# A fused decoder block in float32 on one core: the second feed-forward's output product by seven block products of 2x2 blocks, and two of the four weight sums of each block made by accumulating transfers

## The chip, the cores and the metric

The kernel runs on one core of one Trainium2 chip. The metric is the device time of one execution in microseconds (us). Three timed executions gave 1016.72, 1017.11 and 1018.24 us; the median, 1017.11 us, is the time before.

## What is computed

One decoder layer on 512 positions of width 1024, in float32. Cut to what matters here:

```python
def swiglu(u, w_in, w_out):
    a, b = jnp.split(u @ w_in, 2, axis=-1)
    return (jax.nn.silu(a) * b) @ w_out
...
u = modulate(rmsnorm(h, g_norm_ffn1[l]), sh1, sc1)
h = h + 0.5 * gt1 * swiglu(u, w_ffn1_in[l], w_ffn1_out[l])
u = modulate(rmsnorm(h, g_norm_mix[l]), sh2, sc2)
h = h + gt2 * token_mixing(u, cos, sin, ...)
u = modulate(rmsnorm(h, g_norm_ffn2[l]), sh3, sc3)
h = h + 0.5 * gt3 * swiglu(u, w_ffn2_in[l], w_ffn2_out[l])
return rmsnorm(h, g_final)
```

The nine shifts, scales and gates come from `silu(c) @ w_ada`, 72 blocks of 128 values; VectorE computes most of them beside the first feed-forward and the mixing layer, from transfers of 512 KB. The feed-forward's inner width is 2816, which is 22 inner tiles of 128.

## The kernel before

Everything is kept transposed, features on the 128 partitions and the 512 positions on the free axis. Every operand of a matrix product is split into a high part (the value rounded to the matmul's fp32r format by ScalarE) and a low part (the rest, by VectorE), and each product of 128x128 weights is three matmuls: high by high, high by low and low by high.

**Weights.** They come from HBM in chunks of 128x1024 float32 (512 KB), in one order for the whole kernel (`plan`: the list `loads` says what is transferred, the list `order` in which order chunks are split and used). `fetch` (L215) issues transfers on SyncE's queue (SP) into raw buffers: three (`raw0` to `raw2`), and two more, `rawx`, which are halves of the tile X that become free in the middle of the first block of each feed-forward. `split_hi` (L271) lets ScalarE write the chunk's high part into a ring `whi` (L294); `split_lo` (L300) lets VectorE write the low part into `wlo` (L306) and gives the raw buffer free. The ring holds about seven chunks. `look(4)` (L315) is called ahead of each product and splits chunks up to the fourth one after the chunk that the product takes, so four splits stand in the queues of ScalarE and VectorE ahead of what follows the product.

**The first products of a feed-forward.** `ffn_pair` computes the two halves (a and b) of one inner tile with 24 matmuls of 512 columns each; the first feed-forward does tiles 4 to 7 so (0 to 3 are done at the start), the second tiles 0 to 3 (`PLAIN`). Further tiles go in twos through `duo` (L723), by seven block products in place of eight: the weights of two tiles are four blocks of 128x1024 (W11, W12, W22, W21; each is two tiles by half of the 1024 rows), the input u is cut into four blocks too (half of the rows by half of the positions), and sums of blocks are multiplied. The sums of u are made once (`u_steps`); the sums of weights are made for every block by VectorE, four subtractions of 128x1024 each (`make`, L240). In the list `order` a block of weights is seven entries, called e0 to e6 below. `product` (L712) does one of the seven: 24 matmuls of 256 columns. The products 0, 2, 4 and 6 accumulate in the same PSUM bank A; after product 0 ScalarE copies A to bank C, after products 2 and 4 to SBUF (L726), and the next product into A has to wait for that copy. `step` runs work that was put off (`later`) by a number of products.

**The output of a feed-forward** (`ffn`). The 22 inner tiles are five parts (`PARTS`): four of four tiles and a last one of six. After a part's tiles (and, in most parts, the first duo of the next part, `pairs_before`) the kernel multiplies them by the output weights: four chunks, two of the eight output tiles each, 96 matmuls of 512 columns, and adds each to H with the gate (L863). In the first feed-forward VectorE works at blocks of `w_ada` beside this (`bg`, L360), and their transfers into the tiles cs and AR stand in SP's queue between those of the weights (L352).

A part of four tiles in the second feed-forward is so two duos of seven products and an output of four chunks. `H`, `HI`/`HK` (high and low part of the inner tiles) and the input's `UH`/`UL` lie in SBUF.

Of the kernel before, what the change touches and what calls it, by code (L numbers as in the profile page):

```python
# [55 lines left out]
def lay_ffn(w_in, w_out, first, plain):  # L56

    ins, outs = [], []  # L60
    if first:
        cols = np.concatenate([c for j in range(first) for c in _tiles(j * P, DFF + j * P)])
        for k in range(KT):
            ins.append(w_in[k * P:(k + 1) * P][:, cols])
    for j in range(first, plain):
        for c in _tiles(j * P, DFF + j * P):
            ins.append(_fmajor(w_in, c))
    for j in range(plain, FT, 2):
        for i, c in ((0, 0), (0, DFF), (1, DFF), (1, 0)):
            rows = w_in[i * D // 2:(i + 1) * D // 2]  # L70
            ins.append(np.concatenate([_fmajor(rows, x) for x in _tiles(c + j * P, c + j * P + P)], axis=1))
    for k0, k1 in PARTS:
        for m in range(KT):
            outs.append(_fmajor(w_out[k0 * P:k1 * P], np.arange(m * P, (m + 1) * P)))
    n = KT * (len(PARTS) - 1)
    return ins, [np.concatenate(outs[i:i + 2], axis=1) for i in range(0, n, 2)] + outs[n:]
# [60 lines left out]
class Kernel:  # L137
# [6 lines left out]
    def plan(self):  # L144
# [21 lines left out]
        def blocks(recs):  # L166
            n = len(self.loads)
            self.shifted.update(range(len(self.order), len(self.order) + 7))
            self.loads.extend(recs)
            r11, r12, r22, r21 = (("raw", n + i) for i in range(4))  # L170
            x0, x1 = ("x", 0), ("x", 1)
            for need, src, make in ((0, r11, None), (1, x0, (x0, r12, r11)), (2, x1, (x1, r22, x0)), (3, r21, None),
                                    (3, r12, (r12, r22, r12)), (3, r22, None), (3, x0, (x0, r21, x1))):
                for j, x in enumerate((r11, r12, r22, r21)):
# [8 lines left out]
        def ffn(n, ins, outs, first):  # L183
# [4 lines left out]
            for part, (k0, k1) in enumerate(PARTS):  # L188
# [9 lines left out]
                plain(outs[part * KT // 2:(part + 1) * KT // 2] if part + 1 < len(PARTS) else outs[-KT:])  # L198
# [16 lines left out]
    def fetch(self, n=None):  # L215

        n = len(self.order) - 1 if n is None else min(n, len(self.order) - 1)
        while self.fetched <= self.order[n][1] and self.free:
            i = self.fetched
            name, off, w = self.loads[i]  # L220
            src = self.a[name][off:off + P * w].rearrange("(p n) -> p n", p=P)
# [12 lines left out]
    def make(self, i):  # L234

        while self.made <= i:
            m = self.order[self.made][3]
            if m:
                out, x, y = (self.source(z) for z in m)
                self.nc.vector.tensor_tensor(out, x, y, op=OP.subtract)  # L240
# [400 lines left out]
    def ffn_post(self, j, s, pb):  # L641
        nc = self.nc
        h = self.fw.tile([P, T], F32, name=("hf", "u3")[j % 2])
# [5 lines left out]
    def ffn_silu(self, j, pa):  # L649
        s = self.fw.tile([P, T], F32, name=("sl", "u2")[j % 2])  # L650
# [22 lines left out]
    def u_steps(self, n):  # L673
# [18 lines left out]
        def whole(u, k):  # L692
# [5 lines left out]
        return ([whole(a11, 0), whole(a12, 4)] if n else []) + [add(a22, a21, a22, OP.add), split(0, a22), add(a21, a11, a21, OP.subtract), split(2, a21),  # L698
                add(a11, a22, a11, OP.subtract), split(1, a11), add(a12, a12, a11, OP.subtract)], last
# [23 lines left out]
    def duo(self, j, first, last):  # L723
# [13 lines left out]
        c = self.fw.tile([P, 2 * T], F32, name="hf")  # L737
        u2, u3, p5 = (self.fw.tile([P, T], F32, name=x) for x in ("u2", "u3", "p5"))
        q = lambda x: x.rearrange("p (j h t) -> p j h t", j=2, h=2)
        r = lambda x: x.rearrange("p (j t) -> p j t", j=2)  # L740
        silu = lambda h, bank: nc.scalar.activation(q(s)[:, :, h, :], r(bank), AF.Silu)
# [4 lines left out]
        def high():  # L746
            copy(self.HHall[:, j % NH * T:(j % NH + 2) * T], c)

        def low():
            x = slice(j % NH * T, (j % NH + 2) * T)  # L750
            v.tensor_tensor(self.HLall[:, x], c, self.HHall[:, x], op=OP.subtract)


        for i, (bank, u, start) in enumerate(((A, blk(lo4, T1), True), (B, S[0], True), (A, S[1], False),
                                              (C, blk(hi4, T1), False), (A, S[2], False), (B, S[3], False),
                                              (A, blk(hi4, T2), False))):
            if i == 6:
                v.tensor_tensor(q(c)[:, :, 1, :], r(u3), r(p5), op=OP.add)
# [8 lines left out]
            elif i == 1:  # L767
                copy(p5, B)
            elif i == 2:
                copy(u2, A)  # L770
            elif i == 3:
                silu(0, C)
            elif i == 4:
                copy(u3, A)
            elif i == 6:
                silu(1, A)
                v.tensor_tensor(q(c)[:, :, 0, :], r(B), r(u2), op=OP.add)
# [8 lines left out]

    def ffn2(self):
        self.put, self.now = [], 0
        bk = [self.nb() for _ in range(4)]
        self.head(2, bk, AF.Silu)  # L790
        self.todo, last = self.u_steps(2)
# [33 lines left out]
    def ffn(self, n, j, last=None):  # L825
# [10 lines left out]
        for part, (k0, k1) in enumerate(PARTS):  # L836
            tail = part + 1 == len(PARTS)
            while j < pairs_before(n, part):
# [3 lines left out]
                else:  # L842
                    self.duo(j, last, tail and j + 2 == FT)
# [5 lines left out]
            hk = [(self.HH[k % NH], self.HL[k % NH]) for k in range(k0, k1)]  # L849
            if not tail:  # L850
# [494 lines left out]
    def build(self):  # L1345
# [39 lines left out]
        with self.open_ffn():  # L1385
            self.ada_pool = ExitStack()
            self.adaw = self.ada_pool.enter_context(tc.tile_pool(name="f1a", bufs=4))
            self.put, self.now = [], 0
# [135 lines left out]
def lay_inputs(x, c, positions, w_ada, b_ada, g_norm_ffn1, w_ffn1_in, w_ffn1_out, g_norm_mix, w_in, w_pool,  # L1524
# [4 lines left out]
    f1i, f1o = lay_ffn(A(w_ffn1_in)[0], A(w_ffn1_out)[0], FIRST, PLAIN[0])  # L1529
    f2i, f2o = lay_ffn(A(w_ffn2_in)[0], A(w_ffn2_out)[0], 0, PLAIN[2])  # L1530
# [33 lines left out]
```

## Time and profile before

| what | value |
|---|---|
| median of three timed executions | 1017.11 us (1016.72 to 1018.24) |
| span of the profiled execution, first to last instruction | 1018.4 us |
| busy: TensorE (PE), VectorE (DVE), ScalarE (ACT), GpSimd (POOL) | 1007.5, 756.1, 437.2, 26.2 us |
| mean granted TensorE clock | 0.997 |
| the second feed-forward, from its first inner tile of 512 columns to the last part | 691 to 973 us |

The profiled execution's own time is its span, 1018.4 us, 0.13% over the median of the timed ones. PE is the row of matmuls; a matmul's busy time overlaps the next one's, so that the spacing of the starts, not the mean duration, is what one costs. In a row of a group stand the line, the engine, the operation, the tiles out<-in, the shapes and the count; then busy us and mean ns; then the idle time of the engine just before them and what ended it. SPq is the queue of transfers that SyncE issues.

### The profile page before, as it was taken

To read this page: it belongs to the slowest core of one execution; us is meant where nothing else is said; L and a number is where in the kernel's file an instruction comes from. 1 tells how busy PE (TensorE), PEld (TensorE's weight loads), DVE (VectorE), ACT (ScalarE), POOL (GpSimd) and SP (SyncE) were. 2 spreads that over 40 slices of the span, in tenths; PEclk is the share of its full clock that TensorE was granted. 3 is DMA by queue.
4 is the path that set the end of the run, shared out by engine and by line. 5 is a ranking of instruction groups with operands and counts; after the bars stand their busy time and mean duration, and the time that the engine had idled before them with its cause. 6 is when DMAs were issued, how large, how long until landed. Compare 5 with 4: busy or idle time off the path is not lost.

```text
span 1018.4 us, 15580 instructions
## 1 busy us (share of the span) xinstructions
PE 1007.5 (99%) x6364; PEld 913.3 (90%) x6364; DVE 756.1 (74%) x1112; ACT 437.2 (43%) x668; POOL 26.2 (3%) x30
## 2 busy tenths in 40 slices
PE   8999999999999999999999999999999999999997
PEld 7888898989999999889988888998899899998997
DVE  6979879889786776879447776577787776676764
ACT  5453352625444552233414323364366254352553
POOL 0000000000000000007100000000000000000001
PEclk9999999999999999999999999999999999999998
DMA  8856465455533413122154773312243234241312
GB/s 314 287 196 246 136 211 176 175 168 174 168 111 112 147 46 104 52 83 83 32 198 167 248 271 121 117 53 78 88 168 123 80 105 145 84 144 44 111 34 83
DMA packets 43114, 139.61 MB, mean 137 GB/s; under 512 B 4897, under 2 KB 8225, under 8 KB 43042
## 3 DMA queue, kind: packets, MB, share of 16 engines
q1 hardware_dynamic: 42354, 137.95, 40.8%
q8 instruction: 50, 0.82, 0.3%
q10 hardware_dynamic: 688, 0.66, 0.2%
q14 instruction: 22, 0.18, 0.1%
HBM read 135.82 MB, written 2.77 MB: 136 GB/s over the span
## 4 chain that ended last, share of the span: by engine, by line
PE 94%; DVE 4%; ACT 0%; issue 0%; DMA 0%; DVEq 0%; ACTq 0%
PE bank L337 17%; PE bank L338 17%; PE bank L339 17%; PE bank L719 10%; PE bank L721 10%; PE bank L720 10%; PE bank L1494 1%; PE bank L1496 1%; PE bank L1498 1%; PE bank L1090 1%; PE bank L1269 1%; PE bank L1423 1%; PE bank L1270 1%; PE bank L1271 1%; PE bank L1038 1%; DVE wlo L306 1%
## 5 line engine op out<-in xcount | busy, mean ns | idle before, releaser
L306 DVE TENSOR_TENSOR wlo<-raw,whi 128x1024 fp32r<-128x1024 f32 (+6 forms) x173 | 177.4, 1037 | 67.6 <-ACT whi L294 67.1
L294 ACT ACTIVATE whi<-raw 128x1024 fp32r<-128x1024 f32 (+6 forms) x173 | 152.3, 899 | 40.6 <-DVE raw L240 39.0
L337 PE MATMUL bank<-UH,whi 128*128 128x512 f32 (+1 forms) x432 | 158.3, 366 | 0.0
L338 PE MATMUL bank<-UL,whi 128*128 128x512 f32 (+1 forms) x432 | 154.2, 357 | 0.1
L339 PE MATMUL bank<-UH,wlo 128*128 128x512 f32 (+1 forms) x432 | 154.1, 357 | 0.0
L337 PE MATMUL bank<-HI,whi 128*128 128x512 f32 (+1 forms) x406 | 146.6, 361 | 0.0
L338 PE MATMUL bank<-HK,whi 128*128 128x512 f32 (+1 forms) x406 | 146.3, 360 | 0.0
L339 PE MATMUL bank<-HI,wlo 128*128 128x512 f32 (+1 forms) x406 | 146.2, 360 | 0.0
L721 PE MATMUL bank<-UH,wlo 128*128 128x256 f32 x512 | 141.6, 277 | 0.0
L719 PE MATMUL bank<-UH,whi 128*128 128x256 f32 x512 | 141.6, 277 | 0.0
L720 PE MATMUL bank<-UL,whi 128*128 128x256 f32 x512 | 141.6, 277 | 0.0
L306 DVE TENSOR_TENSOR wlo<-X,whi 128x1024 fp32r<-128x1024 f32 (+4 forms) x96 | 105.3, 1103 | 39.0 <-ACT whi L294 38.7
L719 PE MATMUL bank<-SH,whi 128*128 128x256 f32 x384 | 107.1, 279 | 0.1
L720 PE MATMUL bank<-SL,whi 128*128 128x256 f32 x384 | 107.0, 279 | 0.0
L721 PE MATMUL bank<-SH,wlo 128*128 128x256 f32 x384 | 106.9, 278 | 0.0
L294 ACT ACTIVATE whi<-X 128x1024 fp32r<-128x1024 f32 (+4 forms) x96 | 89.9, 958 | 32.1 <-DVE X L240 28.9
L720 PEld LDWEIGHTS bank<-UL,whi 128*128 128x128 f32 x512 | 96.3, 188 | 0.3
L719 PEld LDWEIGHTS bank<-UH,whi 128*128 128x128 f32 x512 | 96.1, 188 | 0.3
L721 PEld LDWEIGHTS bank<-UH,wlo 128*128 128x128 f32 x512 | 96.1, 188 | 0.0
L339 PEld LDWEIGHTS bank<-UH,wlo 128*128 128x128 f32 x432 | 81.3, 188 | 12.1
L338 PEld LDWEIGHTS bank<-UL,whi 128*128 128x128 f32 x432 | 81.2, 188 | 11.7 <-issue 0.5
L337 PEld LDWEIGHTS bank<-UH,whi 128*128 128x128 f32 x432 | 81.2, 188 | 11.3 <-issue 0.5
(225 smaller groups left out, 1746.4 us busy)
## 6 DMA issues: line engine op xcount, KB each, us to landing
ada<-wada SPq DMA_DIRECT2D x47, 512.0 KB, 5.0
raw<-wmix SPq DMA_DIRECT2D x44, 512.0 KB, 3.6
raw<-wf1i SPq DMA_DIRECT2D x34, 512.0 KB, 4.3
raw<-wf2i SPq DMA_DIRECT2D x30, 512.0 KB, 3.5
X<-wf2i SPq DMA_DIRECT2D x14, 512.0 KB, 3.6
cs<-wada SPq DMA_DIRECT2D x12, 512.0 KB, 3.5
AR<-wada SPq DMA_DIRECT2D x12, 512.0 KB, 4.0
raw<-wf2o SPq DMA_DIRECT2D x12, 512.0 KB, 3.6
```

The source lines that it names most:

```text
L294: self.nc.scalar.activation(self.hi[:, y], r[:, x], AF.Copy)
L306: self.nc.vector.tensor_tensor(self.lo[:, y], r[:, x], self.hi[:, y], op=OP.subtract)
L337: M(ps, hi, uh, start=start, stop=False)
L338: M(ps, hi, ul, start=False, stop=False)
L339: M(ps, lo, uh, start=False, stop=stop)
L719: M(o, hi, uh, start=start and p == 0 and k == 0, stop=False, skip_group_check=True)
L720: M(o, hi, ul, start=False, stop=False, skip_group_check=True)
L721: M(o, lo, uh, start=False, stop=k == 3, skip_group_check=True)
L1038: M(S[:, o + i * P:o + i * P + P], qz[:, (2 * i + h) * P:(2 * i + h + 1) * P], k[:, toks], start=True, stop=True)
L1090: M(o, pt[:, blk * P:blk * P + P], v, start=i == 0, stop=i == len(srcs) - 1)
L1269: M(b, self.UH[k][:, c::4], hi, start=k == 0, stop=False)
L1270: M(b, self.UH[k][:, c::4], lo, start=False, stop=False)
```

## The change

Three things are changed.

1. In the second feed-forward the output of the four parts of four tiles is computed as a block too (`out_quad`): the output weights of four inner tiles by four output tiles are blocks of 128x1024 (`quads` in `lay_ffn`), seven entries of `order` per part, and each of the seven products is 24 matmuls of 256 columns, 168 a part. The sums of the inner tiles are made by `h_sums` during the duo ahead of it, from float32 copies that are kept in the tiles cond, cs and AR. The next part's first duo now comes ahead of the output of the first part too (`pairs_before`).
2. Of a block's four weight sums two are made by transfers: W12 is loaded, and W11 is then added to it in the raw buffer by an accumulating transfer that GpSimd issues (`t1` below; the data of W11 was loaded for e0 already and is read again); W12 is loaded a second time and W22 added (`t3`). VectorE keeps two sums. The signs of the sums change with it. A block is now five loads and two accumulating transfers in place of four loads. This holds for the blocks of both feed-forwards.
3. The temporary tiles of `duo` are laid out differently, and where a duo's second half is split by `h_sums`, the duo splits the first half alone.

```diff
     def blocks(recs):
-        self.loads.extend(recs)
-        r11, r12, r22, r21 = (("raw", n + i) for i in range(4))
+        w11, w12, w22, w21 = recs
+        self.loads.extend((w11, w12 + w11[:2], w22, w21, w12 + w22[:2]))
+        r11, t1, r22, r21, t3 = (("raw", n + i) for i in range(5))
         x0, x1 = ("x", 0), ("x", 1)
-        for need, src, make in ((0, r11, None), (1, x0, (x0, r12, r11)), (2, x1, (x1, r22, x0)), (3, r21, None),
-                                (3, r12, (r12, r22, r12)), (3, r22, None), (3, x0, (x0, r21, x1))):
+        for need, src, make in ((0, r11, None), (1, t1, None), (2, x1, (x1, t1, r22)), (3, r21, None),
+                                (4, t3, None), (4, r22, None), (4, x0, (x0, x1, r21))):
...
     def fetch(self, n=None):
...
             for c in self.pieces(i, w):
-                self.nc.sync.dma_start(self.buf[i][:, c], src[:, c])
+                self.nc.sync.dma_start(self.buf[i][:, c], at(name, off)[:, c])
+            if more:
+                self.nc.gpsimd.dma_start(self.buf[i], at(*more), accum_op=OP.add)
...
-    return k1 if part + 1 == len(PARTS) or (n == 2 and part == 0) else k1 + 2
+    return k1 if part + 1 == len(PARTS) else k1 + 2
...
+    def h_sums(self, k0):
...
+        for n, what in enumerate(((lambda: add(h22, h21, h22, OP.subtract), lambda: high(0, h22)),
+                                  (lambda: add(h21, h11, h21, OP.subtract), lambda: high(2, h21), lambda: low(0, h22)),
+                                  (lambda: add(h11, h22, h11, OP.subtract), lambda: high(1, h11), lambda: low(2, h21)),
+                                  (lambda: add(h12, h12, h11, OP.add), lambda: high(3, h12), lambda: low(1, h11)),
+                                  (lambda: low(3, h12),))):
+            for f in what:
+                self.later(2 + n, f)
+
+    def out_quad(self, k0, gate):
...
+        def product(banks, u, start):
+            w = self.take()
+            for m in range(4):
+                o = banks[m // 2][:, m % 2 * HT:m % 2 * HT + HT]
+                for k in range(2):
+                    (hi, lo), (uh, ul) = w[2 * m + k], u[k]
+                    M(o, hi, uh, start=start and m % 2 == 0 and k == 0, stop=False, skip_group_check=True)
+                    M(o, hi, ul, start=False, stop=False, skip_group_check=True)
+                    M(o, lo, uh, start=False, stop=k == 1, skip_group_check=True)
...
+        for i, (bank, u, start) in enumerate(((A, blk(k0, T1), True), (B, G[0], True), (A, G[1], False),
+                                              (C, blk(k0 + 2, T1), False), (A, G[2], False), (B, blk(k0, T2), False),
+                                              (A, blk(k0 + 2, T2), False))):
+            if i == 6:
+                for b in range(2):
+                    v.tensor_tensor(D[b][:, :, 1, :], p5[b], D[b][:, :, 1, :], op=OP.subtract)
+            self.look(4)
+            product(bank, u, start)
+            self.step()
+            for b in range(2):
+                if i == 0:
+                    copy(C[b], A[b])
+                elif i == 1:
+                    copy(p5[b], r(B[b]))
+                elif i == 2:
+                    copy(D[b][:, :, 0, :], r(A[b]))
+                elif i == 3:
+                    for m in (2 * b, 2 * b + 1):
+                        to_h(m, C[b][:, m % 2 * HT:m % 2 * HT + HT], T1)
+                elif i == 4:
+                    copy(D[b][:, :, 1, :], r(A[b]))
+                elif i == 5:
+                    v.tensor_tensor(D[b][:, :, 0, :], r(B[b]), D[b][:, :, 0, :], op=OP.subtract)
...
     def ffn(self, n, j, last=None):
...
+                    if self.kept and not tail and j == k1:
+                        self.h_sums(k0)
                     self.duo(j, last, tail and j + 2 == FT)
...
+            if not tail and n:
+                self.out_quad(k0, gate)
+                continue
```

How the first block of the first feed-forward stands on ScalarE before (the block's weights are split by L294; raw2 is W21, raw0 is W12 after VectorE's sum; bank0<-bank4 is the copy of A to C after product 0; in brackets the semaphores waited for, DMAHW those of SP's transfers):

```order
L646 ACTIVATE HI_118<-u3_976 128x512 [waits DVE_49]
L294 ACTIVATE whi_69<-raw2_68 128x1024 [waits DMAHW1_49,Activation_49]
L294 ACTIVATE whi_69<-raw0_66 128x1024 [waits DVE_49,Activation_49]
L726 ACTIVATE bank0_97<-bank4_101 128x512 [waits PE_49,Activation_49]
L688 ACTIVATE UH_81<-X_120 128x4x256
L294 ACTIVATE whi_69<-raw1_67 128x1024 [waits DMAHW5_49]
```

And the same place on ScalarE with the change (lines have new numbers: L306 is the high part, L738 the copy; DMASW are the semaphores of GpSimd's transfers):

```order
L658 ACTIVATE HI_118<-u3_976 128x512 [waits DVE_49]
L306 ACTIVATE whi_69<-raw2_68 128x1024 [waits DMAHW0_49,Activation_49]
L306 ACTIVATE whi_69<-raw0_66 128x1024 [waits DMASW1_49,Activation_49]
L738 ACTIVATE bank0_97<-bank4_101 128x512 [waits PE_49,Activation_49]
L700 ACTIVATE UH_81<-X_120 128x4x256
L306 ACTIVATE whi_69<-raw1_67 128x1024 [waits DMAHW5_49]
```

Nothing has moved, but the third row, the high part of e4, waited for VectorE's sum and now waits for the second accumulating transfer, t3.

SP's queue around the same block with the change (L234 are the base loads of the weights, in turn W12 for t1, W22, W21, W12 for t3, and the first output chunk; L364 are blocks of `w_ada`):

```order
L234 DMA raw0_66<-wf1i 128x1024 [waits DMAHW4_49,DMAHW1_49,DVE_49]
L234 DMA raw1_67<-wf1i 128x1024 [waits DMAHW2_49,DVE_49]
L364 DMA cs_93<-wada 128x1024 [waits DMAHW6_49,DVE_49]
L364 DMA AR_86<-wada 128x1024 [waits DMAHW7_49,DVE_49]
L234 DMA raw2_68<-wf1i 128x1024 [waits DMAHW3_49,Activation_49]
L364 DMA cs_93<-wada 128x1024 [waits DVE_49]
L364 DMA AR_86<-wada 128x1024 [waits DVE_49]
L234 DMA raw0_66<-wf1i 128x1024 [waits DMASW0_49,Activation_49]
L234 DMA raw0_66<-wf1o 128x1024 [waits DMAHW4_49,DMASW1_49,DVE_49]
```

The row before the last is new: t3's base load goes into the buffer that held t1 and stands behind two loads of `w_ada`.

ScalarE at the first block of the second feed-forward with the change (raw2 is t1 in the first row and t3 in the rows of 896 and 128 columns, X is the sum of e2, raw1 is W21; cs is an inner tile; bank4<-bank2 is the copy of A to C after product 0):

```order
L306 ACTIVATE whi_69<-raw2_68 128x1024 [waits DMASW6_49]
L663 ACTIVATE p5_6000<-bank0_97 128x512 [waits PE_49,Activation_49]
L306 ACTIVATE whi_69<-X_5610 128x1024 [waits DVE_49]
L658 ACTIVATE HI_5608<-cs_93 128x512 [waits DVE_49]
L306 ACTIVATE whi_69<-raw1_67 128x1024 [waits DMAHW7_49]
L306 ACTIVATE whi_69<-raw2_68 128x896 [waits DMASW7_49]
L306 ACTIVATE whi_69<-raw2_68 128x128
L738 ACTIVATE bank4_101<-bank2_99 128x512 [waits PE_49,Activation_49]
```

This block stood behind the first part's output before; now it stands right behind inner tile 3, and the copy to C stands behind the split of t3 here too.

More of the change, by code (lines that the diff above doesn't have):

```diff
@@ L197, in ffn @@
                         j, at = j + 2, at + 4
-                plain(outs[part * KT // 2:(part + 1) * KT // 2] if part + 1 < len(PARTS) else outs[-KT:])
+                put = blocks if n and part + 1 < len(PARTS) else plain
+                put(outs[part * KT // 2:(part + 1) * KT // 2] if part + 1 < len(PARTS) else outs[-KT:])
         ffn(0, f1i, f1o, FIRST)
```

94 lines of the change are left out of this document (73 added, 21 removed).

## Prediction

> **What bounds the kernel now.** I read the page's head and chain first, then PE's waits, then busy time by stage.
>
> ```profile
> span 1018.4 us, 15580 instructions
> PE 1007.5 (99%) x6364; PEld 913.3 (90%) x6364; DVE 756.1 (74%) x1112; ACT 437.2 (43%) x668; POOL 26.2 (3%) x30
> ...
> PE 94%; DVE 4%; ACT 0%; issue 0%; DMA 0%; DVEq 0%; ACTq 0%
> ```
>
> The matmuls fill the span and the chain that ended last runs 94% on PE.
>
> ```profile
> PE bank L1416 <- ACT cond L1414: 3.3, 1, 3.3
> PE bank L1067 <- ACT prob L1055: 0.3, 1, 0.3
> PE bank L423 <- ACT ut L490: 0.3, 1, 0.3
> ```
>
> This is all of PE's waits, none of them in a feed-forward's blocks. So a matmul removed is time gained, and a wait given to PE is time lost at its full length. The stages of the second feed-forward, by windows (us, then PE, PEld, DVE, ACT, POOL busy with counts, granted clock, DMA share, GB/s): one output, the two duos behind it, and an output with two duos of the first feed-forward.
>
> ```profile
> 792.67:814.45 21.78, 21.78 (x98) 18.03 (x97) 15.19 (x17) 6.72 (x8) 0.00 (x0) 1.00 0.19 58
> 814.45:852.98 38.53, 38.53 (x337) 38.52 (x336) 28.07 (x29) 20.04 (x27) 0.00 (x0) 1.00 0.41 135
> 208.14:268.80 60.66, 60.60 (x435) 56.64 (x433) 53.69 (x72) 26.78 (x35) 0.00 (x0) 1.00 0.54 174
> ```
>
> **What the change removes.** An output is 96 matmuls of 512 columns in 21.78 us (the counts in the rows hold one or two neighbours). Two duos are 336 matmuls of 256 columns in 38.53 us, 19.27 us a block of seven products. A block as the output costs PE the same, 168 like matmuls, so each of four outputs falls from 21.78 to 19.27 us: 4 x 2.51 = **10.05 us less**. That is less than the eighth that seven products for eight suggest, since 256 columns cost more than half of 512 (0.1147 against 0.2269 us a matmul).
>
> In the first feed-forward VectorE loses two of four sums per block, some 1.14 us each. PE gains by that only where it waited for VectorE, and over all outputs and duos there I find one such place:
>
> ```profile
> 240.98 0.28 PE L721 MATMUL bank<-UH,wlo 128*128 128x256 f32 x1
> 241.31 0.39 PE L719 MATMUL bank<-SH,whi 128*128 128x256 f32 x1
> ```
>
> 0.33 us in place of 0.115 between starts, and a slow first matmul: about **0.35 us** with the next one. Gain in all: 10.4 us.
>
> **What hides the added work, and what it costs without cover.** VectorE in the second feed-forward: 15.19 + 28.07 = 43.3 us of 60.31 before. Per part it gets three more low parts and two more sums in the output (5 x 1.14), loses four sums in the duos (4 x 1.14), and gets eight operations of 512 columns from `h_sums` (8 x 0.61, less 0.5 for the half it saves), four more adds of 512 (2.4) and 0.6 for smaller steps into H: 8.5 us more, 51.8 of 57.8 us, 90%. The row 208.14 to 268.80 had 53.69 of 60.66, 89%, and cost PE the 0.35 us. So I put this at nothing, up to 8 us (2 us a part) if it lags. ScalarE gets 3 chunks and copies, far from full.
>
> The uncertain piece is **the time of an accumulating transfer**, A, from the landing of the base load to its own landing. No transfer of GpSimd and no accumulation is in the trace; the nearest rows are plain loads of the same 512 KB, count, KB, and us to landing:
>
> ```profile
> raw<-wf1i SPq DMA_DIRECT2D x34, 512.0 KB, 4.3
> raw<-wf2i SPq DMA_DIRECT2D x30, 512.0 KB, 3.5
> ...
> q1 hardware_dynamic: 42354, 137.95, 40.8%
> ```
>
> 40.8% of 16 engines over 1018.4 us by 42354 packets is 0.157 us a packet; 512 KB are 128 packets of 4 KB, eight an engine, 1.3 us. An accumulation also reads what it adds to. I take A = 3.5 + 1.3 for the second read + 0.5 chosen for GpSimd's issue = **5.3 us** (an estimate). Ends: 3.5, as a plain load; 7.0, two plain loads in series. The Trainium skill, "DMA: Bandwidth & Descriptors", section "Anatomy of one DMA — SWDGE (gpsimd) path", has 2.0 us plus bytes by 436 GB/s for a plain transfer from GpSimd, 3.2 us here; no run here shows it, and the sum below would come out at 1014 us by it.
>
> In steady blocks A is hidden. A buffer comes free with the low part of e6 some 3 us into product e2 (sum, high and low part), and t3 of the next block is split from the start of product e7, five products of 2.75 us behind e2: 10.7 us, of which a base load takes 3.5. Then 3.9 us are left until ScalarE's copy behind that split is late for PE (2.75 + 2.75 less 1.0 and 0.6). So PE waits only when A is over 11 us.
>
> **The first block of each feed-forward is different.** There only three raw buffers exist, t3 must go into t1's buffer, and the split of t3 stands ahead of the copy of A to C, without which product 2 can't start. In the first feed-forward that place reads:
>
> ```profile
> 125.98 1.22 DVE L360 SCALAR_TENSOR_TENSOR AR<-AR,cond 128x1024 f32<-128x1024 f32 x1
> 127.24 0.33 SPq L352 DMA_DIRECT2D AR<-wada  x1
> 128.50 0.28 PE L719 MATMUL bank<-UH,whi 128*128 128x256 f32 x1
> 132.01 1.07 ACT L294 ACTIVATE whi<-raw 128x1024 fp32r<-128x1024 f32 x1 [1.00 <-DVE raw L240]
> 132.97 0.58 ACT L726 ACTIVATE bank<-bank 128x512 f32<-128x512 f32 x1
> 134.21 0.28 PE L719 MATMUL bank<-SH,whi 128*128 128x256 f32 x1
> ```
>
> Today the split of e4 starts at 132.01, the copy ends at 133.55, product 2 starts at 134.21: 0.66 us to spare. With the change t3's base load stands in SP's queue behind the load into AR, so it starts at 127.6 and lands at 131.9 (4.3 us). The accumulation lands at 131.9 + A, the copy ends 1.54 us later and PE starts 0.1 us behind it: product 2 waits 131.9 + A + 1.64 less 134.21, about A - 0.65 = **4.65 us**.
>
> In the second feed-forward the first block moves to where the first output stands:
>
> ```profile
> 711.60 0.69 DVE L647 TENSOR_TENSOR HK<-hf,HI 128x512 fp32r<-128x512 f32 x1 [0.70 <-ACT HI L646]
> 711.47 1.05 ACT L294 ACTIVATE whi<-raw 128x1024 fp32r<-128x1024 f32 x1
> 712.41 0.58 ACT L651 ACTIVATE u<-bank 128x512 f32<-128x512 f32 x1
> 713.18 0.39 PE L337 MATMUL bank<-HI,whi 128*128 128x512 f32 x1
> ```
>
> VectorE is at 712.2 when it can make x1 (1.14) and the low part of t1 (1.14), which ends at 714.6 with ScalarE's part. Then t3's base load starts in that buffer, lands at 718.1, the accumulation at 718.1 + A; copy 1.54 us later and PE's start 0.1 behind it: 719.75 + A. The block begins at 713.18, and product 2 would start 5.71 us later by the rows above, at 718.9. Wait: A + 0.85 = **6.15 us**.
>
> Behind it follows a block at once (the first output). The t1 of that output goes into a half of X that comes free with `first()`, some 4.0 us after t3 has landed (split, copy, high and low part of S3, with a low part between); + 3.5 + A until t1 has landed, + 2.3 for the split, an inner tile's high part and the copy of u3 that stands behind them on ScalarE: A + 9.8. Product 6 of the duo, which needs that copy, is due 12.7 us after t3's landing: 1.64 us until product 2 starts, and four products of 2.75 us (11.0). Wait: A - 2.9 = **2.4 us**. The first feed-forward has a plain output there, whose loads carry no A. Waits in all: 13.2 us.
>
> **The clock.** PE has not stood still so long before. What happens to it when it does shows only at the end:
>
> ```profile
> 1010.00:1012.50 2.50, 1.61 (x12) 1.23 (x11) 0.59 (x2) 1.04 (x3) 0.00 (x0) 1.00 0.11 36
> 1012.50:1018.40 5.90, 0.00 (x0) 0.00 (x0) 1.75 (x5) 0.00 (x0) 1.41 (x2) 0.50 0.53 178
> ```
>
> With PE idle the granted clock is 0.50, for the 5.9 us that are left. So a long wait can be followed by matmuls at half speed: between nothing and, if half clock lasts as long as here, 3 us a wait. I take 1.5 us for each of the two waits over 4 us: **3.0 us**. The Trainium skill, "TensorE: Matmul & The Clock Gate", section "What's actually happening", says that an idle window of about 3.4 us halves the clock and that about 3.4 us of activity restores it: the trace agrees as to the fall, and by it two waits cost 3.4 to 6.8 us in place of my 3.0.
>
> **Sum**: -10.4 + 13.2 + 3.0 = +5.8 us, on a span 1.3 us over the median of the runs; laid on the median, **1022.9 us**. In A: three waits grow by 3 us for each us of A, so break-even, without clock, is A = 4.4 us. At A = 3.5 it is 7.8 us of waits and no clock, 1014.5; at A = 7.0, 18.3 us of waits and up to 9 for the clock, 1025 to 1034.
>
> **Rivals.**
> - *The first-block waits don't come* (t3 is ready early, or PE has other cover): 1006.7 us. For it: everything else hides, and steady blocks have 7 us for A. Against it: three buffers and the order of ScalarE and SP, which leave 0.66 us.
> - *Every block waits*: the accumulation takes over 11 us and from there each of 18 later blocks pays the excess. At 11 us the first blocks alone give 3 x 5.7 = 17.1 more waits than at 5.3 and the clock 9 in place of 3: 1046 us, and at 13 (three waits 2 us longer, 18 blocks of which each pays 2 us) some 1088. Against it: plain loads land in 3.5 us. For it: GpSimd's issue is in no row. A mechanism would be that GpSimd gets its turn only between VectorE's operations, which at 90% busy stand back to back for tens of us. The Trainium skill, "SBUF — State Buffer", section "Who interferes with whom", has such a lock for VectorE's two-port operations, but says that `tensor_tensor` doesn't take it.
> - *VectorE becomes the bound* of the second feed-forward: +2 us a part, 1031 us with the forecast's waits. Against it the 89% stretch that cost 0.35 us.
> - *The output's block does not get 19.27 us*: an output tail of 256 columns spaces them at 0.1188 us (below); 4 x 168 x 0.0041 = 2.8 us less gain, 1025.7.
>
> ```profile
> 649.34:661.81 12.47, 12.47 (x107) 12.46 (x105) 7.88 (x12) 6.36 (x10) 0.00 (x0) 1.00 0.44 143
> ```
>
> **How the numbers follow.** Forecast with A between 3.5 and 7: 0.55, own range 1014.5 to 1034. No first-block waits: 0.15. Every block waits: 0.17. VectorE: 0.08. Dearer output block: 0.05. The range takes in the first and the forecast and leaves out the late transfers: 1006.5 to 1036. 0.2%, some 2 us, is about what a measurement of this kernel can tell from no change. Faster by more: 0.15 and 0.09 of the forecast (A under 3.9), 0.24; within: 0.09 (A up to 4.6 without clock); slower: the rest, 0.67.
>
> **What would show it.** Right: PE waits in the product 2 of each feed-forward's first block, for ScalarE's copy, behind a split that waits for GpSimd's transfer, 4 to 7 us long, a third wait in the first output; outputs of 19.3 us; no waits of over 0.5 us in later blocks. Wrong: transfers of GpSimd that land in under 3.5 us or over 8, waits in every block, a clock of 1.00 right behind a 5 us wait.

## The result, and the profile after

The changed kernel takes **1064.04 us** (median of four, 1061.95 to 1064.87) against 1017.67 us for the kernel before in the same comparison: ratio 1.0449, 95% interval 1.043 to 1.0468. The forecast was 1022.9 us, the range ended at 1036, so the sign was right and the size wrong by 41 us.

The head of the page and all of PE's waits of over a microsecond with the changed kernel (engine, tile, line, who was waited for: us in total, times, longest):

```profile
span 1061.9 us, 16423 instructions
PE 1011.6 (95%) x6652; PEld 929.1 (87%) x6652; DVE 770.9 (73%) x1166; ACT 474.4 (45%) x730; POOL 61.0 (6%) x70
...
PE 69%; DMA 12%; DVE 11%; issue 4%; ACT 3%; SPq 0%; DVEq 0%; POOLq 0%; ACTq 0%
```

```profile
PE bank L731 <- ACT u L738: 22.4, 10, 4.4
PE bank L731 <- ACT bank L738: 16.9, 4, 7.4
PE bank L1530 <- ACT cond L1528: 3.3, 1, 3.3
```

Before, PE had no such wait in a block; now there are 14, 39.3 us, all for a copy by ScalarE (L738) in a duo. The chain that ended last was 94% PE; now transfers and VectorE hold 23% of it. By windows of the changed kernel (us, then PE, PEld, DVE, ACT, POOL busy with counts, granted clock, DMA share, GB/s), the first duo and a later pair of the first feed-forward, then the first duo, a block output and two later pairs of the second:

```profile
125.98:152.89 26.91, 21.70 (x169) 21.48 (x168) 14.72 (x15) 12.26 (x16) 1.73 (x2) 0.87 0.67 201
174.68:218.22 43.54, 39.55 (x338) 38.95 (x336) 31.71 (x37) 19.82 (x26) 2.60 (x3) 1.00 0.70 212
730.23:767.34 37.11, 24.26 (x169) 23.65 (x168) 22.31 (x26) 15.52 (x21) 3.47 (x4) 0.82 0.61 156
767.34:786.38 19.04, 19.04 (x170) 19.04 (x169) 16.03 (x22) 12.29 (x18) 0.87 (x1) 1.00 0.72 190
786.38:830.80 44.42, 40.59 (x339) 40.20 (x337) 33.96 (x41) 23.52 (x32) 3.49 (x4) 0.96 0.64 168
849.84:895.09 45.25, 41.16 (x338) 40.90 (x337) 33.95 (x41) 23.43 (x32) 4.12 (x5) 0.92 0.65 165
```

The output is what it was meant to be, 19.04 us in place of 21.78. Everything lost is in duos: 26.91 in place of 19.33, 37.11 in place of 19.27, pairs of 43.5 to 45.8 in place of 38.5 (the last pair of each feed-forward has no wait and takes 38.5 and 38.4). Where two neighbouring starts of matmuls stand over 0.5 us further apart than usual, the excess sums to 41.6 us (15.2 in the first feed-forward, 26.4 in the second). (The view of waits counts each from the modelled end of the last matmul, 0.17 us less a wait, hence its 39.3 us.) Seven stretches of matmuls at about twice the usual spacing, each behind one of these waits, cost 14.5 us more (3.8 and 10.7). With four outputs 11.0 us shorter this makes +45.1 us. The span grew by 43.5, since this execution's start was 2.5 us shorter than the other's (first tile of 512 columns at 60.71 against 63.22 us), in a part that the change does not touch: at the start matmuls of 128 columns stand 0.21 us apart, and this spacing halves at 11.9 us here and at 19.3 us in the other execution. (Device time is not span: this execution's is 1063.66 us, 1.8 over its span, so spans are compared with spans alone.)

The first block of the first feed-forward, of which the prediction said most (GpSimd's accumulating transfer for t3, then ScalarE's split of it and copy of A to C, then PE's next matmul):

```profile
129.93 0.86 POOL L236 DMA_DIRECT2D raw<-wf1i  x1 [21.60 <-DVE wlo L318]
...
135.47 1.06 ACT L306 ACTIVATE whi<-raw 128x1024 fp32r<-128x1024 f32 x1 [6.98 <-DMA raw<-wf1i]
136.43 0.58 ACT L738 ACTIVATE bank<-bank 128x512 f32<-128x512 f32 x1
...
137.06 0.58 PE L731 MATMUL bank<-SH,whi 128*128 128x256 f32 x1 [5.21 <-ACT bank L738]
```

This is the forecast mechanism: 5.5 us from GpSimd's issue to the split that waited for it, and a wait of 5.21 us where 4.65 were forecast. What was not forecast is the rest.

### The profile page after: what moved, and what is told of

Read it like the earlier page. It is cut to its first block, busy times and chain, and to the rows that moved or that the text cites. A ratio compares the mean times of both kernels' runs of the same rounds, so it can differ in the third digit from the quotient of the medians.

```text
span 1061.9 us, 16423 instructions
## 1 busy us (share of the span) xinstructions
PE 1011.6 (95%) x6652; PEld 929.1 (87%) x6652; DVE 770.9 (73%) x1166; ACT 474.4 (45%) x730; POOL 61.0 (6%) x70
## 3 DMA queue, kind: packets, MB, share of 16 engines
q0 software_dynamic: 5760, 20.97, 11.6%
## 4 chain that ended last, share of the span: by engine, by line
PE 69%; DMA 12%; DVE 11%; issue 4%; ACT 3%; SPq 0%; DVEq 0%; POOLq 0%; ACTq 0%
PE bank L349 13%; PE bank L350 13%; PE bank L351 13%; PE bank L731 5%; PE bank L733 5%; PE bank L732 5%; DMA X<-wf2i 4%; DVE wlo L318 3%; DMA X<-wf1i 3%; DMA AR<-wada 2%; PE bank L859 2%; PE bank L858 2%; PE bank L857 2%; PE bank L1608 1%; PE bank L1610 1%
## 5 line engine op out<-in xcount | busy, mean ns | idle before, releaser
L318 DVE TENSOR_TENSOR wlo<-raw,whi 128x1024 fp32r<-128x1024 f32 (+5 forms) x183 | 189.6, 1048 | 76.4 <-ACT whi L306 74.5
L306 ACT ACTIVATE whi<-raw 128x1024 fp32r<-128x1024 f32 (+5 forms) x183 | 163.6, 909 | 52.7 <-DMA raw<-wf1i 31.1
L318 DVE TENSOR_TENSOR wlo<-X,whi 128x1024 fp32r<-128x1024 f32 (+5 forms) x100 | 107.6, 1084 | 69.4 <-ACT whi L306 69.3
L731 PE MATMUL bank<-SH,whi 128*128 128x256 f32 x384 | 114.1, 297 | 32.7 <-ACT bank L738 16.9
L731 PEld LDWEIGHTS bank<-SH,whi 128*128 128x128 f32 x384 | 78.2, 204 | 34.7 <-ACT bank L738 17.7
L306 ACT ACTIVATE whi<-X 128x1024 fp32r<-128x1024 f32 (+5 forms) x100 | 92.1, 941 | 29.1 <-DMA X<-wf1i 12.4
L731 PEld LDWEIGHTS bank<-UH,whi 128*128 128x128 f32 x512 | 97.0, 189 | 7.6 <-ACT u L738 7.3
L349 PE MATMUL bank<-HI,whi 128*128 128x512 f32 (+1 forms) x278 | 96.8, 348 | 0.0
L350 PE MATMUL bank<-HK,whi 128*128 128x512 f32 (+1 forms) x278 | 96.5, 347 | 0.0
L351 PE MATMUL bank<-HI,wlo 128*128 128x512 f32 (+1 forms) x278 | 96.4, 347 | 0.0
```

What stands on the lines that cost most here:

```text
L306: self.nc.scalar.activation(self.hi[:, y], r[:, x], AF.Copy)
L318: self.nc.vector.tensor_tensor(self.lo[:, y], r[:, x], self.hi[:, y], op=OP.subtract)
L349: M(ps, hi, uh, start=start, stop=False)
L350: M(ps, hi, ul, start=False, stop=False)
L351: M(ps, lo, uh, start=False, stop=stop)
L731: M(o, hi, uh, start=start and p == 0 and k == 0, stop=False, skip_group_check=True)
```

## The experiments

Waits and clock below are, for each kernel's profiled execution, the two sums of the result's section (excess over the usual spacing at waits; extra spacing in slow stretches), for the first and the second feed-forward. In the changed kernel they are 15.2 + 3.8 and 26.4 + 10.7 us. The kernel before has none.

**1. All sums by VectorE, output by blocks.** Part two of the change undone:

```diff
-            self.loads.extend((w11, w12 + w11[:2], w22, w21, w12 + w22[:2]))
+            self.loads.extend(recs)
...
-                                (4, t3, None), (4, r22, None), (4, x0, (x0, x1, r21))):
+                                (3, r12, (r12, r22, r12)), (3, r22, None), (3, x0, (x0, r21, x1))):
```

> The output by block products stays, all four weight sums of a block are VectorE's again (four loads, no accumulating transfer). Theory T (the loss is PE's waits behind the accumulating transfers, 41.6 us, and the half clock behind the long ones, 14.5 us; the block output itself gains 11 us): both go, and what is left is 1017.7 - 11 = 1006.7 us, plus what VectorE lacks: 51.3 us of work per part in the changed kernel (33.96 + 17.32) and 6 more sums of 1.14 us are 58.1 us in 57.4 us of PE, 0.7 us a part, so 1006 to 1012 us. Rival V (VectorE's added work for the sums of inner tiles is what makes the later blocks of the second feed-forward wait): with still more work on VectorE these waits, 13 us and their clock, stay or grow: over 1022 us.

Measured 1034.17 us, ratio 1.0166 (1.0146 to 1.0186). The first feed-forward has no wait; the second still has 18.2 + 7.9 us, without a single accumulating transfer. Theory T alone falls here. What holds PE shows in VectorE's and ScalarE's rows of a duo (L819 is VectorE's sum of inner tiles, L822 ScalarE's high part of it, L737 the duo's copy, L305 and L317 the high and low part of a weight chunk):

```profile
786.20 0.69 DVE L819 TENSOR_TENSOR cond<-AR,cond 128x512 f32<-128x512 f32 x1
789.02 1.23 DVE L317 TENSOR_TENSOR wlo<-X,whi 128x1024 fp32r<-128x1024 f32 x1 [2.13 <-ACT whi L305]
790.17 0.68 DVE L819 TENSOR_TENSOR AR<-AR 128x512 f32<-128x512 f32 x1
...
794.12 0.69 DVE L819 TENSOR_TENSOR AR<-cond,AR 128x512 f32<-128x512 f32 x1
```

```profile
786.92 0.63 ACT L822 ACTIVATE ut<-cond 128x512 fp32r<-128x512 f32 x1 [2.86 <-DVE cond L819]
787.46 0.58 ACT L737 ACTIVATE p<-bank 128x512 f32<-128x512 f32 x1
787.94 1.05 ACT L305 ACTIVATE whi<-X 128x1024 fp32r<-128x1024 f32 x1
790.88 0.63 ACT L822 ACTIVATE ut<-AR 128x512 fp32r<-128x512 f32 x1 [1.89 <-DVE AR L819]
791.42 0.58 ACT L737 ACTIVATE u<-bank 128x512 f32<-128x512 f32 x1
```

Read the two engines in turn. VectorE's sum at 786.20 lets ScalarE's high part start (786.92, after 2.86 us of waiting); the copy (787.46) and the next weight's high part (787.94) stand behind it; VectorE has waited 2.13 us for that high part when it makes the low part (789.02), and only behind this stands its next sum (790.17). One round is 790.17 - 786.20 = 3.97 us, the next 3.95, and each holds one product that PE does in 2.75 us. Neither engine is short of time: each waits for the other once a round. Four rounds stand in every duo ahead of a block output. Each is 1.2 us longer than PE's product, and PE waits as soon as the lead that the two engines had over it is used up.

**2. The transfers alone.** Output of the second feed-forward plain again, the blocks' accumulating transfers kept:

```diff
-                put = blocks if n and part + 1 < len(PARTS) else plain
+                put = plain
...
-            if not tail and n:
+            if False:
                 self.out_quad(k0, gate)
```

> The accumulating transfers stay in both feed-forwards, the second feed-forward's output is plain again (96 matmuls of 512 columns, no sums of inner tiles, the first duo behind the first output as in the kernel before). Theory T: the first feed-forward loses what it loses in the changed kernel (19.6 us), the first block of the second waits at product 2 for 5 to 8 us with 2 to 3 us of clock, the later blocks there do not wait, since a transfer chain of 5.2 + 7.4 us from the free buffer fits the 14 us that there are and no sum of inner tiles stands ahead of ScalarE's copies: 1017.7 + 19.6 + 9 = 1046 us, 1042 to 1050. Rival D (accumulating transfers are late for every block whatever else runs): the three later pairs lose 6 us each as now, about 1065 us.

Measured 1046.29 us, ratio 1.0279 (1.0259 to 1.0299): theory T's number, though not all of its terms. The first feed-forward loses 13.6 + 1.5 (forecast 19.6), the second 8.9 + 2.9 (forecast 9), all in its first block; its later blocks do not wait. In that first block the long wait, 7.5 us, is not at product 2 (1.4 us) but at product 6, whose copy stands behind the split of the next block's t1: that base load starts at 757.4 and the accumulation ends at 772.0 us.

```profile
PE bank L731 <- ACT bank L738: 10.7, 4, 5.6
PE bank L731 <- ACT u L738: 10.5, 4, 7.3
```

The two parts add up: +16.5 us for the first experiment and +28.6 for this one are +45.1; both together, the change, are +46.4.

**3 and 4. A fourth raw buffer.** A smaller ring makes room (the control), then the buffer is added for the time of each feed-forward:

```diff
-RING = 7 * 1024 + 128
+RING = 6 * 1024 + 640
...
+        self.more = [fp.tile([P, CW], F32, name=f"more{i}") for i in range(1)]
...
+            self.free += self.more
             self.startup()
...
             self.sums, self.retired = self.open_sums(), []
+            self.free += self.more
```

> Control for the next run: the changed kernel with a ring of 6784 columns for the split weights in place of 7296, which frees 4 KB a partition. Six chunks fit it, which is what the four chunks of lookahead need: the changed kernel's time, 1059 to 1067 us, by every theory.

> As the run before, and the 4 KB are a fourth raw buffer in both feed-forwards. Theory T: the base load of t3 no longer needs the buffer that t1 leaves or the half of X that e6 leaves late, but the one that e0 leaves, some two products (5.5 us) earlier. The waits of product 2 in the two first blocks (5.4 and 7.6 us) go to 0 to 2, those of later blocks (25 us) too, and the clock with them: 1007 to 1018 us. Rival V: the waits in the second feed-forward's later blocks stay, 13 us and 6 us of clock: 1026 us or more. Rival D (the added 21 MB slow all transfers): waits fall little, over 1045 us.

The control takes 1065.41 us (two runs, ratio 1.0465, 1.0436 to 1.0494), the changed kernel's time. With the buffer: 1044.73 us, ratio 1.0266 (1.0238 to 1.0293). That is far over theory T's range and fits rival V's "1026 us or more", and each was right in its place: the first feed-forward falls from 15.2 + 3.8 to 4.9 + 0 us, the wait of its first block is gone; the second keeps 22.6 + 8.5, with two waits of up to 2.4 us in each later pair, the rounds of the first experiment. In its first block product 2 still waits 4.8 us: in the chain VectorE's sums of u and the low parts behind them end at 714.6, and only then t3's base load starts there. Rival D's bound, 1045 us, is missed by 0.3 us alone, so this run doesn't rule D out; experiment 10 does.

**5. Only the order on ScalarE.** The changed kernel with each high part of an inner tiles' sum one product later (and the low part behind it):

```diff
-            for f in what:
-                self.later(2 + n, f)
+            self.later(2 + n, lambda o=o, x=x, y=y, op=op: add(o, x, y, op))
+            self.later(3 + n, lambda i=i, o=o: high(i, o))
+            self.later(4 + n, lambda i=i, o=o: low(i, o))
```

> The changed kernel with one order changed: the high part that ScalarE makes of each sum of inner tiles comes one product after VectorE's sum, not right behind it, and the low part one later too. Theory P (in the second feed-forward's later blocks ScalarE waits for a sum at the end of VectorE's queue, the copies and the next weight split stand behind that wait, and VectorE's next sum behind that split: a round of 3.96 us against 2.75 us of PE): the round is broken, the waits of the later pairs, 13 us, and their clock, 6.3 us, go for the most part: 1040 to 1048 us. Rival T (those waits are the late accumulating transfers): under 4 us less, 1058 us or more. Rival B (VectorE is simply full): as T's.

Measured 1043.2 us (1039.08 to 1051.43, ratio 1.026, 1.0223 to 1.0296): theory P's number, 20.8 us less by the medians for the same instructions in another order. The second feed-forward falls from 26.4 + 10.7 to 15.0 + 4.1 us, of which 13.2 + 4.1 are its first block: 18.0 us of the 20.8 can be counted where the edit acts. The first feed-forward, which the edit doesn't touch, had 10.2 + 3.7 here against 15.2 + 3.8; its waits change that much from one profiled execution to another.

**6. That order without transfers.** Experiment 1 with the order of experiment 5.

> The first experiment (all weight sums by VectorE, output by block products) with the high parts one product later. Theory P: of its 27.5 us over 1006.7 only the first block of the second feed-forward stays, where VectorE's queue is late (a wait of 3.0 us and 1.5 us of clock): 1008 to 1014 us, faster than the kernel before. Rival B (VectorE is full: 18.93 of 19.00 us in the block output, 22.93 of 23 us behind the duos): the waits only move, 1025 us or more.

Measured 1014.92 us, ratio 0.9963 (0.9947 to 0.9979), 19.3 us less than experiment 1, 0.9 us over theory P's range. (In its profiled execution the spacing at the start halves only at 19.9 us, in experiment 1's at 11.5, so that its first duo begins 3.2 us later for no reason of the edit: 128.86 against 125.67 us.) Two waits in blocks are left, and the windows of a pair of duos and of the block output behind it show VectorE (third pair of numbers) without a gap:

```profile
PE bank L730 <- ACT bank L737: 2.9, 1, 2.9
PE bank L730 <- ACT u L737: 0.5, 1, 0.5
```

```profile
759.21:797.60 38.39, 38.39 (x338) 38.39 (x337) 38.32 (x45) 24.54 (x34) 0.00 (x0) 1.00 0.33 110
797.60:816.65 19.05, 19.05 (x171) 19.05 (x169) 19.02 (x25) 11.18 (x17) 0.00 (x0) 1.00 0.37 112
```

VectorE is busy 57.34 of 57.44 us and PE waits for nothing. So rival B falls, and with it a reading that busy shares invite: the kernel with VectorE at 81% of a part (51.28 of 63.46 us, the changed one) waited, the one at 99.8% did not.

**7 and 8. One transfer per block in place of two**, with the later high parts. In 7 W22 is added to W12 in place, once VectorE has made W12 + W11 from it; in 8 the transfer makes t1 and VectorE makes W12 + W22 as the difference of e2's sum and W11.

```diff
-            for need, src, make in ((0, r11, None), (1, t1, None), (2, x1, (x1, t1, r22)), (3, r21, None),
-                                (4, t3, None), (4, r22, None), (4, x0, (x0, x1, r21))):
+            for need, src, make in ((0, r11, None), (1, x0, (x0, r12, r11, OP.add, w22)), (2, x1, (x1, r22, x0)), (3, r21, None),
+                                    (3, r12, None), (3, r22, None), (3, x0, (x0, r21, x1))):
...
+                if len(m) > 4:
+                    name, off, w = m[4]
+                    self.nc.gpsimd.dma_start(x, self.a[name][off:off + P * w].rearrange("(p n) -> p n", p=P), accum_op=OP.add)
```

```diff
+            self.loads.extend((w11, w12 + w11[:2], w22, w21))
...
+                                    (3, r11, (r11, x1, r11, OP.subtract)), (3, r22, None), (3, x0, (x0, x1, r21))):
```

> One accumulating transfer per block in place of two: W12 is loaded once, VectorE makes W12+W11 from it, and only then W22 is added to W12 in its own buffer by GpSimd's transfer. High parts one product later. Theory T (accumulating transfers are late because t3's base load needs a buffer that comes free late, not because an accumulation of 5.5 to 7.5 us is long in itself): the transfer has three products, 8.2 us, and nothing loads in front of it; the first feed-forward loses under 3 us: 1004 to 1014 us. Rival L (an accumulation takes too long for any place): waits in every block, over 1030 us.

> One accumulating transfer per block, the other one: t1 = W12 + W11 is made by the transfer, W12+W22 by VectorE as the difference of the sum behind e2 and W11, in W11's buffer. High parts one product later. Theory T: t1's base load has the buffer that it had before, so the accumulation is 5.5 to 7.5 us on top of a load that was some products early; only the first blocks wait, 0 to 3 us each: 1005 to 1016 us. Rival L: over 1030 us.

Experiment 7: **1009.26 us, ratio 0.9923 (0.9905 to 0.9941)**, faster than both kernels, 0.8% under the one before. One wait in a block is left in the whole kernel, at product 2 of the second feed-forward's first block:

```profile
PE bank L734 <- ACT bank L741: 1.8, 1, 1.8
```

Its transfers are not quicker than those of the changed kernel (issue to landing, in medians by group, 5.7 to 8.2 us); they start as soon as e1's sum is made, three entries ahead of e4, with no load in front of them. Experiment 8: 1017.95 us, ratio 1.0003 (0.9987 to 1.0018). It has 0.6 us in the first feed-forward and 7.4 + 3.0 in the second, of which 5.5 + 3.0 are one wait in its first block: there the t1 of the first output is loaded into a half of X (issued at 721.0, its accumulation from 727.2 to 734.0). In later blocks it has no wait; the time is 2 us over theory T's range, by that wait. Rival L falls in both.

**9. Experiment 7 with the changed kernel's order.**

> The version with one transfer into W12's own buffer, but with the changed kernel's order of ScalarE's high parts, right behind each sum. Theory P: the round of 3.96 us a product comes back in the three later pairs and in the second half of the first block, whatever the transfers do: 2.4 to 3 us of waits a pair, 3 in the first block, 1.5 us of clock each: 15 to 22 us more than 1009 us, 1024 to 1031 us. Rival T (the round matters only where a transfer is late): 1009 to 1014 us.

Measured 1032.61 us, ratio 1.016 (1.0142 to 1.0178), 23.4 us over experiment 7 and just over theory P's range; the second feed-forward has 18.3 + 6.4 us, as experiment 1 (18.2 + 7.9), although here a transfer makes one sum and there none:

```profile
PE bank L734 <- ACT u L741: 15.0, 8, 2.8
PE bank L734 <- ACT bank L741: 1.8, 1, 1.8
```

**10. Both causes taken away with two transfers kept**: the fourth buffer of 4 and the order of 5.

> Two accumulating transfers per block as in the changed kernel, with the fourth raw buffer (and the smaller ring) and the later high parts together. If the late base load and the order on ScalarE are the two causes and act apart: 1044.7 us less what the order was worth without transfers, 19 us (1034.2 - 1014.9): 1022 to 1030 us, with what stays in the first block of the second feed-forward (5 us of wait and 2 of clock) and three waits of 1 to 2 us in the first feed-forward. If two transfers a block are too many for other reasons (the added 21 MB): over 1035 us.

Measured 1026.72 us, ratio 1.0106 (1.0081 to 1.0132). The waits: 3.7 us in the first feed-forward, 9.8 + 3.3 in the second, nearly all in its first block. The expectation's sum of the two gains, 1025.7 us, is met, so the causes act apart, and the bound of 1035 us for the added 21 MB is not reached. What two transfers still cost in that first block has two places: product 2 waits 4.6 us behind a base load that starts when VectorE's low part has freed the buffer (715.8 us), and product 6 waits 4.6 us behind the accumulation for the first output's t1, which took 10.3 us (733.4 to 743.8).

## Why the prediction was wrong, step by step

- **The output as blocks**, forecast -10.05 us: 4 x (21.78 - 19.04) = -11.0 us. Right.
- **A and the first blocks.** A was put at 5.3 us; the two first blocks show 5.5 us from GpSimd's issue. Product 2 waited 5.21 and 7.38 us for 4.65 and 6.15 forecast, as described: three buffers, t3 behind t1, the copy behind the split. Product 6 of the second feed-forward's first duo waited 3.62 for 2.4, and product 4 there 1.85 more, by the rounds. The mechanism is shown by experiment 4 for the first feed-forward (a buffer, and its wait is gone).
- **"In steady blocks A is hidden"** failed in the first feed-forward (9.8 us of excess behind its first block). The prediction allowed 10.7 + 3.9 = 14.6 us from the free buffer to the copy that PE needs. The chain that ends in PE's wait at 204.5 us takes longer and starts later (start, us, what):

```profile
176.75 4.70 DMA AR<-wada
...
182.70 1.21 DVE wlo L318 x2
183.91 1.14 DVE X L252
185.04 1.15 DVE wlo L318
...
186.59 8.46 DMA X<-wf1i
195.04 0.34 issue
195.39 7.42 DMA X<-wf1i
...
203.97 0.49 ACT bank L738
```

  A transfer for `w_ada` holds VectorE, so its low part frees the buffer at 186.2, 3 us after the point that the prediction counted from (174.68 + 5.5 + 3.0 = 183.2); the base load takes 8.46 us and not 3.5, and the accumulation ends 16.6 us after the buffer was free. The load's time was read as a median, and that of the second feed-forward (3.5 us; the same rows have 4.3 for the first's), and the accumulation's was put together from the same median. Here the two run beside each other and beside `w_ada`'s, and plain loads got slower too (`raw<-wf1i` 5.8 us as a median, 4.3 before). The groups of accumulations:

```profile
raw<-wf1i POOLq DMA_DIRECT2D x9, 512.0 KB, 8.1
...
X<-wf2i POOLq DMA_DIRECT2D x12, 512.0 KB, 6.0
```

  The last pair of this feed-forward (307.62 to 346.15 us) begins behind VectorE's last work on `w_ada` (the last operation starts at 301.8 us) and has no wait; the two accumulations issued from 303 us on took 5.1 and 6.1 us. That fits, but no run took `w_ada`'s work out: its share in these waits is read from the chain, not shown by an experiment. What experiments show is that they shrink with the fourth buffer (4) and vanish with one transfer in place (7).

- **VectorE's added work in the second feed-forward, "I put this at nothing"**, is the step that cost most. The amount was right (51.8 us a part forecast, 51.28 measured), the argument from a busy share of 90% was not: the forecast summed VectorE's time and never set the four sums and their high parts into the two queues. The diff shows the order before any run: `h_sums` puts the high part right behind the sum, at the same product, and the copy and the next weight split then stand behind the high part on ScalarE. The order is worth 20.8 us in the changed kernel (experiment 5), 19.3 without transfers (6 against 1) and 23.4 with one (9 against 7); by the waits and the slow stretches of the second feed-forward alone it is 18 to 21 us each time. In the changed kernel's later pairs the chain to such a wait also runs through an accumulation (8.1 us, for the wait at 884.3 us), but a pair waits about as long there, 4.2 to 4.6 us, as without any accumulation (3.0 to 4.8 in experiment 1); with the transfers and without the sums of inner tiles (2) no later block waits, and with the transfers and the later high parts (5) 1.8 us are left, in one pair.
- **The clock**, forecast 3.0 us for two waits: seven waits were followed by slow matmuls, 1.6 to 2.75 us each, 14.5 in all.
- **The sum**: -10.4 + 13.2 + 3.0 forecast, -11.0 + 41.6 + 14.5 found.
- **The rivals.** "Every block waits" had the time (1046 and more) and named the first feed-forward's later blocks rightly, but by an A of over 11 us, which no row of the changed kernel shows. "VectorE becomes the bound" had the right engine and stage and the wrong mechanism: experiment 6 has it busy throughout at no cost. A round between two queues, which is what happened, was not among the rivals.

Open: `w_ada`'s part in the first feed-forward's later waits, as said; these waits vary between executions (15.2 and 10.2 us with the same instructions there), and what varies was not traced; and the wait that is left in the second feed-forward's first block (1.8 us in experiment 7) was read from VectorE's queue but not tried.

## What to carry to other kernels

When work is put into two in-order queues that feed each other, write out one period of both queues and add up the round (here 0.70 + 0.54 + 0.48 + 1.08 + 1.15 us, the steps from one sum to the next): if it is longer than the period of the engine that they serve, that engine waits, however idle both are, and moving one instruction by a period can be worth more than the work itself. A transfer that needs a buffer another one leaves is priced from the buffer's release, with the durations of that stage, not from a median. And a sum that a transfer is to make belongs into a buffer that is loaded anyway, started as soon as its last reader is done.

## What the runs showed of the hardware

The clock falls after shorter waits than expected, and not after all of them. In experiment 9 one wait of 2.36 us was followed by matmuls at about half clock and one of the same length by matmuls at full clock:

```profile
787.66:790.02 2.36, 0.16 (x2) 0.00 (x0) 2.36 (x4) 1.17 (x3) 0.00 (x0) 1.00 0.00 0
790.02:793.74 3.72, 3.72 (x19) 3.72 (x20) 3.33 (x5) 1.83 (x3) 0.87 (x1) 0.55 0.35 40
850.06:852.42 2.36, 0.17 (x3) 0.00 (x1) 2.36 (x4) 1.17 (x3) 0.00 (x0) 1.00 0.00 0
852.42:856.10 3.68, 3.68 (x32) 3.68 (x33) 3.29 (x5) 1.79 (x3) 0.86 (x1) 1.00 0.38 43
```

The same 3.7 us hold 19 matmuls in one case and 32 in the other. Over all runs (waits as excess over the usual spacing) none of up to 1.94 us was followed by slow matmuls, those from 1.97 to 2.65 us sometimes, all from 2.86 us on; each that was cost 1.5 to 3.0 us.

What separates the two cases is where a wait lies in time. In these traces the granted clock changes on a grid of 3.41 us: in experiment 9 it falls to half at 718.71, 728.95, 790.39 and 923.51 us, whole numbers of 3.41 us apart, and every half-clock stretch in the two feed-forwards of any run is one, two or three such steps long. Adding up PE's waiting inside each step at full clock, over all runs, I find the next step at half clock in all 39 cases with 1.98 us or more, and at full clock in every case with 1.96 us or less. The first wait above lies inside one step (786.98 to 790.39 us); the second is cut by the end of a step at 851.84 us into 1.8 and 0.6 us. The Trainium skill, "TensorE: Matmul & The Clock Gate", section "What's actually happening", gives an idle window of about 3.4 us; the traces have a step of that length, but 2 us of waiting inside it are enough, and the measurement decides.

An accumulating transfer of 512 KB took 5.5 us from issue to landing for t3 of the two first blocks, with no load issued beside it. Elsewhere in the changed kernel's feed-forwards it took 5.1 to 9.3 us, in experiments 4 and 10 up to 10.4 and 10.3 (the first output's t1). Its packets were slower than those of plain loads: 11.6% of 16 engines over 1061.9 us by 5760 packets is 0.34 us a packet, against 0.157 before.

```profile
q0 software_dynamic: 5760, 20.97, 11.6%
```
